# Seven products of halves for eight of the 22 tiles of the up product, and low parts made by an adding DMA

## The chip, the cores and the metric

One core of one Trainium2 chip runs the whole kernel, one layer of a network on 512 positions of 1024 features. The metric is the device time of one execution in microseconds. The kernel before and the changed one are compared by the median of several runs on the same chip. Engines are named as in the profile: PE is TensorE, DVE VectorE, ACT ScalarE, POOL GpSimd, SP SyncE.

## The reference

All is float32. The part that is changed is the first product of the convolutional gated MLP (`h @ w_up`), which is the longest stage of the layer:

```python
x1 = x + rmsnorm_post_mix(W_out(sig(a_ret) * W_ret_o(retention(h)) + sig(a_sgu) * W_sgu_o(sgu(h))))
y  = x1 + rmsnorm_post_ffn(conv_gated_mlp(rmsnorm_pre_ffn(x1)))

def _conv_gated_mlp(h, w_up, conv_w, conv_b, w_down):      # h: 512 x 1024
    hid = h @ w_up                                         # 512 x 5632
    hid = depthwise_conv(hid, conv_w, width=3, pad=1) + conv_b   # along the positions
    a, b = jnp.split(hid, 2, axis=-1)                      # 2 x 2816
    return (jax.nn.gelu(a) * b) @ w_down                   # 2816 x 1024
```

## The kernel before

**Numbers in two parts.** A float32 product is taken in three passes of TensorE: each operand `a` is split into a high part `ah` (a copy in the format that TensorE reads) and a low part `al = a - ah`, and `mm3` adds `ah*bh`, `ah*bl` and `al*bh` in PSUM. The high copy is made by ACT (`copy`), the subtraction by DVE (`split`).

**Weights.** All weights lie in one array `wall` of 146 blocks of 128 x 1024 (512 KB each), in the order of their use. The list `units` says in which form each is needed. `w_get` hands out the next unit and, as it does, prepares units further on (`w_unit`, with `LOOK` as the reach): it loads the block into one of 4 `raw` tiles by a DMA of SP's queue and makes the parts in one of 9 slots of the pool `w4`. A plain block (`w_block`) takes two slots, `wh` and `wl`: an ACT copy 128x1024 and a DVE subtraction 128x1024.

**Products of halves.** For two products of the first half of the kernel (U and the gates), and for the down product, a product of 2 x 2 blocks is taken in seven products of halves instead of eight, with sums and differences of the operands in place of the operands (the algorithm of Strassen in Winograd's form). `w_form` makes the seven forms of weights (B11, B21, T1 to T4, B22, each 128x512 with its two parts): T1 and T3 are sums on DVE, T2 and T4 sums on POOL. `x_forms` makes the forms S1 to S4 of the activations. The class `Pair` takes the seven products, in three parts between which other products can stand, with 84 matmuls 128x256 and three accumulators.

**The up product.** Its 5632 features are 44 blocks of 128, in 22 tiles `i` of two blocks (`e = 2i` of `a`, `2i + 1` of `b`). `f_block` computes one block: 8 slices `k` of the input times 3 passes, 24 matmuls 128x512 into one PSUM bank. `conv` takes the bank with one ACT step (`cv`, the middle tap and the bias) and two DVE steps (the taps of the neighbours), `gated` takes the gelu on ACT and the product `gp` on DVE. After every second tile up to the thirteenth, `down_forms` makes the forms of two `gp` for the down product: eight DVE steps of differences and splits.

**The start of the stage.** The 512 positions are handled as four groups `t` of 128. `norms(t)` computes the rows `x1` and their normalised `xn`; `turn(t)` transposes them (`transpose`, 8 on PE), and writes for each `k` 128 columns of the operand: `h2h` by ACT straight from PSUM, `h2l` by one DVE step from PSUM and `h2h`. The first four blocks are computed in halves of 256 positions (`early(e, 0)` and `early(e, 1)`), the first half before the last two turns are there.

**Order.** The program lists the operations in the order of the text; a scheduler then arranges each engine's queue, so that operations of several stages stand mixed. An engine runs its queue in order and waits for semaphores. The DMA queues are SP's (all weight blocks) and POOL's (`x1` written and read).

The plain split and the whole weight block, as they stand:

```python
    def split(hi, lo, src):
        copy(hi, src)
        nc.vector.tensor_sub(lo, src, as32(hi))
```

Of the kernel before, what the change touches and what calls it, by code (L numbers as in the profile page):

```python
# [12 lines left out]
AF = mybir.ActivationFunctionType  # L13
ALU = mybir.AluOpType

P = 128
# [17 lines left out]
DP = 9  # L34
WHOLE = NF - 2 * DP
EAGER = 7

PRE, FFNG, LNG, LNB = 0, 8, 16, 24
CW, CB = 32, 32 + 3 * 2 * NF
# [4 lines left out]
def tile_block(ctx: ExitStack, tc, xT, x, wall, par, cs, decay, wsp, bsp, gpost, gffn, out):  # L44
# [11 lines left out]
    def blk(dt=F32, n="blk", shape=(P, S)):  # L56
        return sb.tile(list(shape), dt, tag="blk", bufs=NBLK, name=nm(n))

    def tmp(n="tmp", shape=(P, S)):
        return sb.tile(list(shape), F32, tag="tmp", bufs=6, name=nm(n))  # L60
# [16 lines left out]
    def as32(t):  # L77
        return t.bitcast(F32)
# [6 lines left out]

    RES1 = NW - 22 - 44
    RES0 = RES1 - RES_OUT
    units = []
    i = 0
    while i < NW:  # L90
        pair = [(f, i) for f in ("B11", "B21", "T1", "T2", "T3", "T4", "B22")]
        if U0 <= i < GATE0:
            units += pair
            i += 2
        elif GATE0 <= i < GATE1:
            units += pair[:4] + [("blk", i + 2)] + pair[4:] + [("blk", i + 3)]
            i += 4
        elif i == DOWN0:
            for _ in range(2):
                pairs = [[("q", i + j), ("t", i + j)] for j in range(DP)]  # L100
                whole = [[("blk", i + DP)], [("blk", i + DP + 1)]]
                for u in pairs[:4] + whole[:1] + pairs[4:6] + whole[1:] + pairs[6:] if i == DOWN0 else pairs + whole:
                    units += u
                i += DP + WHOLE // 2
        else:
            units.append(("blk", i))
            i += 1
# [8 lines left out]
    def w_block(i):  # L116
        raw = raw_tile() if i else raw0
        resident = RES0 <= i < RES1
        if i > 0:
            nc.sync.dma_start(raw, wall[i])  # L120
        if resident:
            hi, lo = [], []
            for c in range(2):
                h_, l_ = blk(F32R, "wh"), blk(F32R, "wl")
                split(h_, l_, raw[:, c * S : (c + 1) * S])
                hi.append(h_)
                lo.append(l_)
        else:
            at = 48 if i >= DOWN0 else 0
            hi, lo = slot("wh", at), slot("wl", at)  # L130
            if i == 0:
                pieces = [slice(0, P), slice(P, S), slice(S, 2 * S)]
                for f in pieces:
                    if f.start:
                        nc.sync.dma_start(raw[:, f], wall[i, :, f])
                    (nc.vector.tensor_copy if f.start == 0 else copy)(hi[:, f], raw[:, f])
                for f in pieces:
                    nc.vector.tensor_sub(lo[:, f], raw[:, f], as32(hi[:, f]))
            else:
                split(hi, lo, raw)  # L140
        return hi, lo
# [21 lines left out]
    def w_down(form, i):  # L163

        if form == "q":
            raw = w_raw["q"] = raw_tile()
            nc.sync.dma_start(raw, wall[i])
            raw = raw[:, : 3 * 256]
        else:
            b, raw = w_raw["q"], raw_tile()  # L170
            two = "p (n c) -> p n c"
            nc.vector.tensor_tensor(
                out=raw[:, :512].rearrange(two, n=2), in0=b[:, :512].rearrange(two, n=2),
                in1=b[:, None, 768:].to_broadcast([P, 2, 256]), op=ALU.add,
            )
            nc.vector.tensor_add(raw[:, 512:768], raw[:, :256], b[:, 256:512])
            nc.vector.tensor_add(raw[:, 768:], raw[:, 512:768], b[:, 512:768])
        w = 768 if form == "q" else 1024
        hi, lo = slot("dh", 48, w), slot("dl", 48, w)
        split(hi, lo, raw)  # L180
        return hi, lo

    def w_unit(u):
        return w_block(u[1]) if u[0] == "blk" else w_down(*u) if u[0] in "qt" else w_form(*u)

    def w_size(u):
        return 2 if u[0] in ("blk", "q", "t") else 1

    def w_get(look=LOOK):

# [29 lines left out]
    def col(i):  # L220
        return part[:, i : i + 1]
# [55 lines left out]
    T0, T1 = slice(0, 256), slice(256, 512)  # L277
    forms = {n: [] for n in ("S1", "S2", "S3", "S4")}

    def x_forms(k):  # L280

        a, b = xg[k], xg[k + 4]
        s_ = blk(n="xs")
        nc.vector.tensor_sub(s_[:, T0], a[:, T1], b[:, T1])
        nc.vector.tensor_sub(s_[:, T1], s_[:, T0], a[:, T0])
        nc.vector.tensor_sub(a[:, T0], a[:, T0], a[:, T1])
        nc.vector.tensor_add(a[:, T1], b[:, T0], s_[:, T1])
        for names, s_ in (("S1", "S2"), s_), (("S3", "S4"), a):
            h_, l_ = blk(F32R, "sh"), blk(F32R, "sl")
            split(h_, l_, s_)  # L290
            for n, t in zip(names, (T0, T1)):
                forms[n].append((h_[:, t], l_[:, t]))
# [344 lines left out]
    class Pair:  # L637


        def __init__(self, func, alloc):  # L640
            self.func, self.t = func, [alloc(), alloc()]
            self.b = [ps() for _ in range(3)]

        def product(self, b, act, first, w=None):
# [9 lines left out]
                    )  # L654
            return o

        @staticmethod
        def x(first, t):
            return lambda k: (xh[first + k][:, t], xl[first + k][:, t])

        @staticmethod
        def s(n):
            return lambda k: forms[n][k]

        def part1(self):
            c0, c1 = self.t
            o = self.product(0, self.x(0, T0), True)
            copy(c0[:, T0], o)
            o = self.product(1, self.x(4, T0), True)
            v.tensor_add(c0[:, T0], o, c0[:, T0])  # L670
            self.product(2, self.s("S1"), True)
            o = self.product(0, self.s("S2"), False)
            copy(c1[:, T0], o)
            v.tensor_mul(c0[:, T0], c0[:, T0], rbc[:, T0])

        def part2(self):
            c0, c1 = self.t
# [5 lines left out]
        def part3(self):  # L683
            c0, c1 = self.t
            o = self.product(0, self.x(4, T1), False, self.w[0])
            v.tensor_mul(c0[:, T1], o, rbc[:, T1])
            nc.scalar.activation(out=c0, in_=c0, func=self.func)
            o = self.product(2, self.s("S4"), False, self.w[1])
            v.tensor_sub(c1[:, T0], o, c1[:, T0])
            v.tensor_mul(c1, c1, rbc)  # L690
            nc.scalar.activation(out=c1, in_=c1, func=self.func)


    nc.sync.dma_start(wst, wsp)
# [5 lines left out]
    copy(rws, rw)  # L700
    uT, late = [], None
    for j in range(KD // 2):
        p = Pair(AF.Gelu_apprx_tanh, lambda: blk(n="u"))
        p.part1()
        if late:
            late.part3()
        p.part2()
        late = p
        uT += p.t
# [32 lines left out]


    def gated_pair(ah, al, late=None):
        p = Pair(AF.Sigmoid, lambda: tmp("sig"))
        p.part1()
        if late:
            late.part3()
        o = [f_block(ah, al, KD)]
        p.part2()  # L750
        o.append(f_block(ah, al, KD, p.part3))
        return zip(o, p.t)
# [64 lines left out]


    gpm = bcast(gpost, "gpm")
    h2h, h2l = [], []  # L820
    x1 = [[dp_.tile([P, S], F32, tag=f"x1_{t}{n}", name=f"x1_{t}{n}") for n in range(2)] for t in range(NT)]
    for k in range(KD):
        h2h.append(blk(F32R, "h2h"))
        h2l.append(blk(F32R, "h2l"))

    def norms(t, acc):

# [26 lines left out]
    def turn(t, zs):  # L854
        c = slice(t * P, (t + 1) * P)
        for n in range(2):
            p = ps()
            for f in range(4):
                nc.tensor.transpose(p[:, f * P : (f + 1) * P], zs[n][:, f * P : (f + 1) * P], ident)
            for f in range(4):  # L860
                k = 4 * n + f
                pf = p[:, f * P : (f + 1) * P]
                nc.scalar.activation(  # L863
                    out=h2h[k][:, c], in_=pf, func=AF.Copy, scale=col(FFNG + k)
                )
                v.scalar_tensor_tensor(
                    out=h2l[k][:, c], in0=pf, scalar=col(FFNG + k), in1=as32(h2h[k][:, c]),
                    op0=ALU.mult, op1=ALU.subtract,
                )

    EARLY = 4
    early_w, early_o = [], []
# [72 lines left out]
            "S3": (th[:, T0], tl[:, T0]), "S4": (th[:, T1], tl[:, T1]),  # L945
        })

    for i in range(NF):
        cc = []
        for s_ in range(2):  # L950
            e = 2 * i + s_
            o = early_o[e] if e < EARLY else f_block(h2h, h2l, KD)
            cc.append(conv(o, e))
        gated(*cc)
        if i % 2 and i // 2 < EAGER:
            down_forms(i // 2)

# [145 lines left out]
def _inter(a, b):  # L1105
    return np.stack([a, b], 1).reshape(2 * a.shape[0], *a.shape[1:])
# [7 lines left out]
    ], 1)  # L1114


def _gates(a, w):

    return np.concatenate([_two(a), _parts(w, 8, P).reshape(4, 2, P, 1024)], 1).reshape(16, P, 1024)
# [79 lines left out]
```

## Time and profile before

| | |
|---|---|
| Three runs | 842.24, 843.88 and 848.6 us, median 843.88 us |
| Profiled execution | 841.63 us, span 839.8 us, mean granted clock 0.997 |
| TensorE busy | 827.2 us (98%) |
| DVE, ACT, POOL busy | 615.1 us (73%), 401.5 us (48%), 76.0 us (9%) |
| DMA | 93.19 MB, mean 111 GB/s |

The span reaches from the first instruction to the last; 1.8 us of the profiled execution's time lie outside it. A row of a group reads: line, engine, operation, output and inputs by name, shapes, count | busy time, mean ns of one | idle time of the engine before them and what ended it. Lines such as L82 belong to a helper (here `split`). A piece of the chain reads: start, length, engine or queue, what, count. In the timeline a row is the start, the duration, the engine and the instruction.

### The profile page before, as it was taken

What the parts mean: (1) busy time and instruction counts of PE and PEld (TensorE: products, weight loads), DVE (VectorE), ACT (ScalarE), POOL (GpSimd) and SP (SyncE); (2) the same over time, 40 slices, a digit from 0 to 9 for tenths busy, and PEclk for the clock granted to TensorE, in tenths of its full rate; (3) what the DMA queues carried; (4) which work ended last, traced back from release to release, by engine and by line L of the source; (5) the groups of instructions that cost most, each with busy time, mean ns of one, the idle gap of its engine ahead of it and who ended that gap; (6) DMA issues with size and microseconds to landing.
All of it is one profiled execution on the core that took longest, in us unless ns stands there. A gap on an engine that the chain in (4) does not pass through costs nothing.

```text
span 839.8 us, 12386 instructions
## 1 busy us (share of the span) xinstructions
PE 827.2 (98%) x4864; PEld 731.3 (87%) x4864; DVE 615.1 (73%) x996; ACT 401.5 (48%) x649; POOL 76.0 (9%) x87
## 2 busy tenths in 40 slices
PE   8999999999999999999999999999999999999995
PEld 6888888888899999999988898888888888999995
DVE  5689898877897776867665767667777556886956
ACT  5635445545664533444444664444444333643531
POOL 0010000102221111132211200000000000000001
PEclk9999999999999999999999999999999999999998
DMA  7733222213233332323457123323222221242532
GB/s 266 265 114 101 76 76 76 75 51 101 87 100 103 101 101 101 101 78 102 149 163 287 66 85 101 101 100 101 97 85 95 100 76 50 80 135 100 159 132 101
DMA packets 29243, 93.19 MB, mean 111 GB/s; under 512 B 3392, under 2 KB 4032, under 8 KB 29184
## 3 DMA queue, kind: packets, MB, share of 16 engines
q1 hardware_dynamic: 26928, 86.85, 31.1%
q0 software_dynamic: 1392, 4.46, 1.5%
q10 hardware_dynamic: 864, 1.09, 0.4%
q8 instruction: 38, 0.62, 0.3%
q14 instruction: 21, 0.17, 0.1%
HBM read 88.19 MB, written 4.19 MB: 110 GB/s over the span
## 4 chain that ended last, share of the span: by engine, by line
PE 96%; DVE 1%; DMA 1%; issue 1%; ACT 0%; POOL 0%; DVEq 0%; SPq 0%; POOLq 0%; ACTq 0%
PE ps L204 16%; PE ps L203 16%; PE ps L205 16%; PE ps L651 14%; PE ps L977 10%; PE ps L465 5%; PE ps L464 5%; PE ps L466 5%; PE ps L798 2%; PE ps L796 2%; PE ps L797 2%; PE ps L993 2%; PE ps L721 1%; DMA raw<-wall 1%; PE ps L264 1%
## 5 line engine op out<-in xcount | busy, mean ns | idle before, releaser
L82 DVE TENSOR_TENSOR wl<-raw,wh 128x1024 fp32r<-128x1024 f32 (+1 forms) x109 | 128.2, 1184 | 100.0 <-PE ps L204 63.7
L205 PE MATMUL ps<-h2h,wl 128*128 128x512 f32 (+1 forms) x384 | 142.3, 371 | 0.0
L204 PE MATMUL ps<-h2l,wh 128*128 128x512 f32 (+1 forms) x384 | 142.2, 371 | 0.0
L203 PE MATMUL ps<-h2h,wh 128*128 128x512 f32 (+1 forms) x384 | 142.2, 372 | 0.0
L75 ACT ACTIVATE wh<-raw 128x1024 fp32r<-128x1024 f32 (+2 forms) x111 | 109.8, 998 | 37.7 <-DMA raw<-wall 18.1
L75 ACT ACTIVATE wf<-raw 128x512 fp32r<-128x512 f32 x84 | 50.8, 627 | 73.5 <-issue 30.2
L203 PEld LDWEIGHTS ps<-h2h,wh 128*128 128x128 f32 x384 | 72.1, 188 | 12.8 <-ACT h2h L863 0.3
L204 PEld LDWEIGHTS ps<-h2l,wh 128*128 128x128 f32 x384 | 72.2, 188 | 12.6
L205 PEld LDWEIGHTS ps<-h2h,wl 128*128 128x128 f32 x384 | 72.2, 188 | 12.3
L82 DVE TENSOR_TENSOR wf<-raw,wf 128x512 fp32r<-128x512 f32 x84 | 65.8, 799 | 19.9 <-ACT wf L75 19.6
L906 ACT ACTIVATE cv<-ps,part 128x512 f32<-128x512 f32 x44 | 34.4, 781 | 87.9 <-PE ps L205 87.9
L464 PE MATMUL ps<-wh,xh 128*128 128x512 f32 x192 | 75.0, 391 | 0.0
L465 PE MATMUL ps<-wl,xh 128*128 128x512 f32 x192 | 74.9, 390 | 0.0
L466 PE MATMUL ps<-wh,xl 128*128 128x512 f32 x192 | 74.8, 390 | 0.0
L651 PE MATMUL ps<-sh,wf 128*128 128x256 f32 x384 | 72.8, 280 | 0.0
L651 PEld LDWEIGHTS ps<-sh,wf 128*128 128x128 f32 x384 | 60.9, 188 | 0.7 <-ACT u L75 0.2
L977 PE MATMUL ps<-dh,fh 128*128 128x256 f32 x216 | 60.3, 279 | 0.0
L977 PE MATMUL ps<-dl,fh 128*128 128x256 f32 x216 | 60.2, 279 | 0.0
L977 PE MATMUL ps<-dh,fl 128*128 128x256 f32 x216 | 60.2, 279 | 0.0
L651 PE MATMUL ps<-xh,wf 128*128 128x256 f32 x288 | 54.6, 281 | 0.0
L651 PE MATMUL ps<-sl,wf 128*128 128x256 f32 x192 | 53.6, 279 | 0.0
L82 DVE TENSOR_TENSOR dl<-raw,dh 128x768 fp32r<-128x768 f32 (+1 forms) x36 | 39.2, 1091 | 18.7 <-PE ps L204 7.9
(290 smaller groups left out, 1851.7 us busy)
## 6 DMA issues: line engine op xcount, KB each, us to landing
raw<-wall SPq DMA_DIRECT2D x145, 512.0 KB, 3.4
x<-x SPq DMA_DIRECT2D x24, 256.0 KB, 5.8
xT<-xT SPq DMA_DIRECT2D x8, 256.0 KB, 5.5
x<-x POOLq DMA_DIRECT2D x8, 256.0 KB, 2.3
xT<-xT POOLq DMA_DIRECT2D x4, 256.0 KB, 3.8
out<-zg SPq DMA_DIRECT2D x4, 256.0 KB, 2.0
out<-zs ACTq DMA_DIRECT2D x3, 256.0 KB, 2.0
cs<-cs SPq DMA_DIRECT2D x2, 256.0 KB, 4.1
```

Source lines behind the costliest of these rows:

```text
L75: nc.scalar.activation(out=o, in_=i, func=AF.Copy)
L82: nc.vector.tensor_sub(lo, src, as32(hi))
L203: nc.tensor.matmul(o, ah, bh, start=start, stop=False)
L204: nc.tensor.matmul(o, ah, bl, start=False, stop=False)
L205: nc.tensor.matmul(o, al, bh, start=False, stop=stop)
L464: nc.tensor.matmul(acc[t], xh[k][:, c], wh[:, f], start=k == 0, stop=False)
L465: nc.tensor.matmul(acc[t], xh[k][:, c], wl[:, f], start=False, stop=False)
L466: nc.tensor.matmul(acc[t], xl[k][:, c], wh[:, f], start=False, stop=k == KD - 1)
L651: nc.tensor.matmul(o, w_[:, c], a_, start=first and k == n == 0, stop=k == 3 and n == 2, skip_group_check=True,)
L796: nc.tensor.matmul(o, ah, bh, start=k == 0, stop=False)
L906: nc.scalar.activation(out=c, in_=o, func=AF.Identity, scale=col(CW + 3 * m + 1), bias=col(CB + m))
L977: nc.tensor.matmul(o, a_[:, c], w_[:, f], start=j == t == i == 0, stop=j == DP - 1 and i == 2 and n not in (M2, M3, M4), skip_group_check= ...
```

## The change

`COUPLES` are the tiles (3, 4), (5, 6) to (17, 18) of the up product. In each, the first tile is one `Pair` with forms of `h2`, a new plain copy of the operand (eight tiles), and the second two `f_block`s, one after the first part of the pair and one after the second. Weights of the first tile are laid out on the host as the four halves (`_up`). The second tile's blocks are `sum` units: ACT copies the high part, ACT writes minus the block into the low tile, and a DMA on POOL's queue adds the block of `wall` onto it. `turn` writes `h2`, and after an odd `t` splits 256 columns of it. `x_forms` runs for four `k` on `h2`. `down_forms` moves to tiles 3, 7, 11, 15, 18, 19 and 20. The classes' scale becomes optional, since the up product has none.

```diff
+UP0 = DOWN0 - 2 * NF
+COUPLES = [(i, i + 1) for i in range(3, 19, 2)]
...
+        elif i == UP0 + 2 * COUPLES[0][0]:
+            for a, b in COUPLES:
+                pair = [(f, UP0 + 2 * a) for f in FORMS]
+                units += pair[:4] + [("sum", UP0 + 2 * b)] + pair[4:] + [("sum", UP0 + 2 * b + 1)]
+            i = UP0 + 2 * COUPLES[-1][1] + 2
...
+    def w_sum(i):
+
+        raw = raw_tile()
+        nc.sync.dma_start(raw, wall[i])
+        hi, lo = slot("wh"), slot("wl")
+        copy(hi, raw)
+        nc.scalar.activation(out=lo, in_=raw, func=AF.Copy, scale=-1.0)
+        nc.gpsimd.dma_start(lo, wall[i], accum_op=ALU.add)
+        return hi, lo
...
-                pf = p[:, f * P : (f + 1) * P]
                 nc.scalar.activation(
-                    out=h2h[k][:, c], in_=pf, func=AF.Copy, scale=col(FFNG + k)
+                    out=h2[k][:, c], in_=p[:, f * P : (f + 1) * P], func=AF.Copy, scale=col(FFNG + k)
                 )
-                v.scalar_tensor_tensor(
-                    out=h2l[k][:, c], in0=pf, scalar=col(FFNG + k), in1=as32(h2h[k][:, c]),
-                    op0=ALU.mult, op1=ALU.subtract,
-                )
+                if t % 2:
+                    d = slice((t - 1) * P, (t + 1) * P)
+                    split(h2h[k][:, d], h2l[k][:, d], h2[k][:, d])
...
-    for i in range(NF):
-        cc = []
-        for s_ in range(2):
-            e = 2 * i + s_
-            o = early_o[e] if e < EARLY else f_block(h2h, h2l, KD)
-            cc.append(conv(o, e))
-        gated(*cc)
-        if i % 2 and i // 2 < EAGER:
-            down_forms(i // 2)
+    def tile_done(i, o):
+        gated(*(conv(t, 2 * i + s_) for s_, t in enumerate(o)))
+        if i < COUPLES[-1][1]:
+            if i % 4 == 3:
+                down_forms(len(dforms))
+        elif len(dforms) < EAGER:
+            down_forms(len(dforms))
+
+    for k in range(4):
+        x_forms(k, h2[k], h2[k + 4], h2forms)
+    couples = dict(COUPLES)
+    i = 0
+    while i < NF:
+        if i in couples:
+            p = Pair(None, lambda: tmp("c"), (h2h, h2l, h2forms))
+            p.part1()
+            o = [f_block(h2h, h2l, KD)]
+            p.part2()
+            o.append(f_block(h2h, h2l, KD, p.part3))
+            tile_done(i, p.t)
+            tile_done(i + 1, o)
+            i += 2
+        else:
+            o = []
+            for e in (2 * i, 2 * i + 1):
+                o.append(early_o[e] if e < EARLY else f_block(h2h, h2l, KD))
+            tile_done(i, o)
+            i += 1
```

More of the change, by code (lines that the diff above doesn't have):

```diff
@@ L87, in tile_block @@
     RES0 = RES1 - RES_OUT
+    FORMS = ("B11", "B21", "T1", "T2", "T3", "T4", "B22")
     units = []
@@ L90, in tile_block @@
     while i < NW:
-        pair = [(f, i) for f in ("B11", "B21", "T1", "T2", "T3", "T4", "B22")]
+        pair = [(f, i) for f in FORMS]
         if U0 <= i < GATE0:
@@ L181, in w_down @@
         return hi, lo
+    def w_sum(i):
[6 more added lines that the diff above has]
+        return hi, lo
     def w_unit(u):
-        return w_block(u[1]) if u[0] == "blk" else w_down(*u) if u[0] in "qt" else w_form(*u)
+        if u[0] in ("blk", "sum"):
+            return (w_block if u[0] == "blk" else w_sum)(u[1])
+        return (w_down if u[0] in "qt" else w_form)(*u)
     def w_size(u):
-        return 2 if u[0] in ("blk", "q", "t") else 1
+        return 2 if u[0] in ("blk", "sum", "q", "t") else 1
     def w_get(look=LOOK):
@@ L278, in tile_block, with x_forms @@
     forms = {n: [] for n in ("S1", "S2", "S3", "S4")}
-    def x_forms(k):
-        a, b = xg[k], xg[k + 4]
+    def x_forms(k, a=None, b=None, forms=forms):
+        a, b = a or xg[k], b or xg[k + 4]
         s_ = blk(n="xs")
@@ L637, in tile_block, with __init__ @@
     class Pair:
-        def __init__(self, func, alloc):
-            self.func, self.t = func, [alloc(), alloc()]
+        def __init__(self, func, alloc, a=None, scale=None):
+            self.func, self.t, self.scale = func, [alloc(), alloc()], scale
+            self.h, self.l, self.forms = a or (xh, xl, forms)
             self.b = [ps() for _ in range(3)]
@@ L655, in product, with x, s @@
             return o
[L657 to L663, printed above, removed]
+        def x(self, first, t):
+            return lambda k: (self.h[first + k][:, t], self.l[first + k][:, t])
+        def s(self, n):
+            return lambda k: self.forms[n][k]
         def part1(self):
@@ L673, in part1 @@
             copy(c1[:, T0], o)
-            v.tensor_mul(c0[:, T0], c0[:, T0], rbc[:, T0])
+            if self.scale is not None:
+                v.tensor_mul(c0[:, T0], c0[:, T0], self.scale[:, T0])
         def part2(self):
@@ L685, in part3 @@
             o = self.product(0, self.x(4, T1), False, self.w[0])
-            v.tensor_mul(c0[:, T1], o, rbc[:, T1])
-            nc.scalar.activation(out=c0, in_=c0, func=self.func)
+            if self.scale is None:
+                copy(c0[:, T1], o)
+            else:
+                v.tensor_mul(c0[:, T1], o, self.scale[:, T1])
+                nc.scalar.activation(out=c0, in_=c0, func=self.func)
             o = self.product(2, self.s("S4"), False, self.w[1])
             v.tensor_sub(c1[:, T0], o, c1[:, T0])
-            v.tensor_mul(c1, c1, rbc)
-            nc.scalar.activation(out=c1, in_=c1, func=self.func)
+            if self.scale is not None:
+                v.tensor_mul(c1, c1, self.scale)
+                nc.scalar.activation(out=c1, in_=c1, func=self.func)
     nc.sync.dma_start(wst, wsp)
@@ L702, in tile_block @@
     for j in range(KD // 2):
-        p = Pair(AF.Gelu_apprx_tanh, lambda: blk(n="u"))
+        p = Pair(AF.Gelu_apprx_tanh, lambda: blk(n="u"), None, rbc)
         p.part1()
@@ L744, in gated_pair @@
     def gated_pair(ah, al, late=None):
-        p = Pair(AF.Sigmoid, lambda: tmp("sig"))
+        p = Pair(AF.Sigmoid, lambda: tmp("sig"), None, rbc)
         p.part1()
@@ L819, in tile_block @@
     gpm = bcast(gpost, "gpm")
-    h2h, h2l = [], []
+    h2h, h2l, h2 = [], [], []
+    h2forms = {n: [] for n in ("S1", "S2", "S3", "S4")}
     x1 = [[dp_.tile([P, S], F32, tag=f"x1_{t}{n}", name=f"x1_{t}{n}") for n in range(2)] for t in range(NT)]
@@ L824, in tile_block @@
         h2l.append(blk(F32R, "h2l"))
+        h2.append(blk(n="h2"))
     def norms(t, acc):
@@ L946, in down_forms @@
         })
-    for i in range(NF):
-        cc = []
-        for s_ in range(2):
-            e = 2 * i + s_
-            o = early_o[e] if e < EARLY else f_block(h2h, h2l, KD)
-            cc.append(conv(o, e))
-        gated(*cc)
-        if i % 2 and i // 2 < EAGER:
-            down_forms(i // 2)
+    def tile_done(i, o):
[19 more added lines that the diff above has]
+            i += 2
+        else:
+            o = []
[3 more added lines that the diff above has]
+            i += 1
     UNITS = (("q", 0, "A11"), ("q", 2, "A12"), ("q", 1, "S4"), ("t", 0, "S1"), ("t", 2, "S2"), ("t", 1, "S3"), ("t", 3, "A22"))
@@ L1114, in _two, with _up @@
     ], 1)
+def _up(a):
+    for i, _ in COUPLES:
+        b, c = a[2 * i].reshape(P, 2, S), a[2 * i + 1].reshape(P, 2, S)
+        a[2 * i : 2 * i + 2] = np.stack([
+            np.concatenate([b[:, 0], c[:, 0]], -1), np.concatenate([c[:, 1], b[:, 1]], -1),
+        ])
+    return a
 def _gates(a, w):
@@ L1166 @@
         _rows(i["w_out"]),
-        _inter(_parts(up[:, :DFF], NF, P), _parts(up[:, DFF:], NF, P)),
+        _up(_inter(_parts(up[:, :DFF], NF, P), _parts(up[:, DFF:], NF, P))),
         _down(i["w_down"]),
```

## The prediction

> **What bounds the kernel now.** I read the page first, then the table of busy time by stretches of 20 us over the stage that is changed, then the chain of waits for the cadence of TensorE.
>
> ```profile
> span 839.8 us, 12386 instructions
> PE 827.2 (98%) x4864; PEld 731.3 (87%) x4864; DVE 615.1 (73%) x996; ACT 401.5 (48%) x649; POOL 76.0 (9%) x87
> PE 96%; DVE 1%; DMA 1%; issue 1%; ACT 0%; POOL 0%; DVEq 0%; SPq 0%; POOLq 0%; ACTq 0%
> ```
>
> TensorE is busy for 98% of the span and makes 96% of the chain that ends last, so only fewer or narrower matmuls, or new holes in PE, can move the time.
>
> ```profile
> core 0: us, PE busy (x) PEld busy (x) DVE busy (x) ACT busy (x) POOL busy (x), PEclk, DMA share, GB/s
> 370.00:390.00 20.00, 20.00 (x127) 18.07 (x126) 14.46 (x21) 8.56 (x15) 5.11 (x5) 1.00 0.28 97
> 480.00:500.00 20.00, 19.98 (x167) 19.74 (x166) 12.78 (x27) 11.47 (x26) 1.69 (x3) 1.00 0.20 61
> 500.00:520.00 20.00, 20.00 (x97) 16.86 (x96) 17.46 (x27) 12.31 (x17) 0.00 (x0) 1.00 0.38 125
> 600.00:620.00 20.00, 20.00 (x90) 16.57 (x89) 14.92 (x22) 9.47 (x13) 0.00 (x0) 1.00 0.28 88
> 720.00:740.00 20.00, 20.00 (x172) 20.00 (x171) 19.97 (x34) 12.71 (x20) 0.00 (x0) 1.00 0.30 93
> ```
>
> The up product is the middle of this table. PE is full there, at the full clock (1.00), DVE has 5 us spare in 20, ACT 10, POOL does nothing and DMA is at 0.28. So there is room to pay for halves with vector work, except at two places: DVE is at 17.46 of 20 where the up product starts and at 19.97 of 20 where it ends.
>
> **What the change removes from PE.** A couple of tiles was 4 blocks of 24 matmuls 128x512. Tile `a` now has 7 products of 12 matmuls 128x256 (84), tile `b` keeps 48 wide ones. The cadence of both kinds:
>
> ```profile
> 368.89 5.66 PE ps L651 x48
> 389.75 5.66 PE ps L651 x48
> 410.60 5.65 PE ps L651 x48
> 501.68 0.40 PE L203 MATMUL ps<-h2h,wh 128*128 128x512 f32 x1
> 719.47 19.79 PE ps L977 x168
> ```
>
> (The first three and the last are pieces of the chain: start, length, what, count; the fourth is the timeline.) Wide: the 40 blocks of 24 between 501.68 and 719.47, 217.8 us / 960 = 0.2269 us. Narrow: 5.66/48 = 0.1179, and 19.79/168 = 0.1178. A couple before is 96 x 0.2269 = 21.78 us. The gate product already runs 84 narrow and 48 wide in turn, and its period is 389.75 - 368.89 = 20.86 us (20.85 for the next). So a couple saves 0.92 by the period, or 84 x 0.1178 + 48 x 0.2269 = 20.79 and 0.99 by the counts. Eight couples: 7.4 to 7.9, taken 7.5 us. That is 0.9% of the time and a ceiling: nothing else leaves PE's queue.
>
> **What it adds in the steady state.** The nearest rows are those of the gate product and of the up product itself.
>
> ```profile
> L82 DVE TENSOR_TENSOR wl<-raw,wh 128x1024 fp32r<-128x1024 f32 x38 | 46.5, 1224 | 60.6 <-PE ps L204 59.5 <-issue 1.0
> L82 DVE TENSOR_TENSOR wf<-raw,wf 128x512 fp32r<-128x512 f32 x75 | 59.7, 812 | 15.7 <-ACT wf L75 15.4
> L155 DVE TENSOR_TENSOR raw<-raw,raw 128x512 f32<-128x512 f32 x10 | 9.1, 909 | 0.7 <-DMA raw<-wall 0.7
> L913 DVE SCALAR_TENSOR_TENSOR cv<-ps,part,cv 128x511 f32<-128x511 f32 x42 | 31.4, 749 | 1.1
> L922 DVE TENSOR_TENSOR gp<-cv,cv 128x512 f32<-128x512 f32 x21 | 14.5, 692 | 0.8
> L936 DVE TENSOR_TENSOR fs<-fs,gp 128x256 f32<-128x256 f32 x7 | 3.0, 425 | 0.2
> L75 ACT ACTIVATE wh<-raw 128x1024 fp32r<-128x1024 f32 x37 | 38.9, 1051 | 0.0
> L906 ACT ACTIVATE cv<-ps,part 128x512 f32<-128x512 f32 x42 | 32.8, 781 | 85.8 <-PE ps L205 85.8
> L75 ACT ACTIVATE wf<-raw 128x512 fp32r<-128x512 f32 x75 | 45.4, 627 | 68.5 <-issue 30.2 <-PE ps L204 21.1 <-PE ps L651 12.8
> L75 ACT ACTIVATE sig<-ps 128x256 f32<-128x256 f32 x24 | 9.0, 377 | 8.3 <-PE ps L651 8.3
> L156 POOL TENSOR_TENSOR raw<-raw,raw 128x512 f32<-128x512 f32 x10 | 18.3, 1832 | 88.3 <-DVE raw L154 63.1 <-DMA raw<-wall 16.9 <-ACT wf L75 4.4
> L158 POOL TENSOR_TENSOR raw<-raw,raw 128x512 f32<-128x512 f32 x11 | 14.2, 1291 | 49.6 <-DVE wf L82 49.6
> ```
>
> DVE, one couple before: 4 `wl` x 1.224 + 8 convolution steps x 0.75 + 2 `gp` x 0.69 + one set of `down_forms` (up to tile 13; eight steps, 5 x 0.42 and 3 x 0.68, 4.1) = 16.4 of 21.78. After: the four `wl` go; 7 `wf` x 0.812, the sums T1 and T3 (0.9 and, by the width, 0.7), 3 combinations 256 wide x 0.42, the same convolution and `gp`, and `down_forms` in every second couple (2.1) = 18.0 of 20.86, 86%. A couple that has its `down_forms` has 20.1. ACT: 7 x 0.627 + 4 x 1.051 (a high and a negated copy for each adding block; the negated one has no row and is priced as `wh`) + 4 x 0.781 + 2 gelu x 0.63 + 4 copies out of PSUM x 0.377 + 1.1 for half a `down_forms` = 15.6, 75%. POOL: 3.1 us of sums and two DMA issues. All of this is covered by PE as long as each form arrives before its product. Walking one couple in the order in which the program issues, the tightest forms (S2's and S3's) come 1.3 to 3.6 us early: priced at 0, and at about 1 us a couple if DVE loses those margins.
>
> **The adding DMA** is in no row. It reads 512 KB of `wall` onto a tile that holds minus the rounded raw block. The nearest rows:
>
> ```profile
> raw<-wall SPq DMA_DIRECT2D x145, 512.0 KB, 3.4
> x<-x POOLq DMA_DIRECT2D x8, 256.0 KB, 2.3
> xT<-xT POOLq DMA_DIRECT2D x4, 256.0 KB, 3.8
> ```
>
> Below: 3.8, a POOL load of half the size. Above: two of these end to end, 7.6, since an add must also fetch what it adds to. I take 5.5. It stands on POOL's queue behind T2 and T4, up to 3.1 us, and its issue. In the walk, ACT ends the negated copy of the first adding block 17.7 us into a couple and PE needs it at 27.0; for the second 25.8 and 33.9. Less POOL, 6.5 to 8 us are left for the landing: no stall at 5.5, at most 1 us each at 7.6. A DMA also lengthens the queue: 6 transfers a couple where 4 were, 3.1 MB in 20.86 us, 151 GB/s, against the 125 that the table shows in the fullest stretch.
>
> The Trainium skill (DMA: Bandwidth & Descriptors, section on the anatomy of a DMA on the gpsimd path) fits 2.0 us plus bytes over 436 GB/s, 3.2 us for 512 KB, and gives no price for the adding kind. The plain load in the trace takes 3.4; by the page the first adding block, below, would stall 0.7 us, not 3.0.
>
> **Where it starts.** Here nothing is spare. Before, each `h2h` is an ACT step straight from PSUM, and DVE's `h2l` follows it, each time 128 columns. Now ACT writes `h2` and, only after the odd `t`, copies 256 columns, so the second turn puts 16 ACT steps where 8 were, and DVE subtracts 256 wide.
>
> ```profile
> 476.63 0.28 PE L203 MATMUL ps<-h2h,wh 128*128 128x256 f32 x1
> 476.89 0.60 ACT L807 ACTIVATE junk<-ps 128x512 f32<-128x512 f32 x1
> 478.13 0.35 DVE L866 SCALAR_TENSOR_TENSOR h2l<-ps,part,h2h 128x128 fp32r<-128x128 f32 x1 [0.36 <-ACT h2h L863]
> 478.50 0.75 DVE L838 SCALAR_TENSOR_TENSOR z<-ps,qr,gpm 128x512 f32<-128x512 f32 x1
> 477.92 0.55 POOL L815 TENSOR_TENSOR qr<-qs,nhalf 128x1 f32<-128x1 f32 x1 [1.66 <-DVE qs L812]
> 489.64 2.73 ACT L863 ACTIVATE h2h<-ps,part 128x128 fp32r<-128x128 f32 x7 [3.93 <-PE ps L859]
> 490.06 0.74 PE ps L203 x4
> ```
>
> (Timeline rows; the last is a piece of the chain.) Four places, each walked from these rows with the new order of instructions:
>
> 1. The first early block starts at 476.63 and takes a slice of `h2` every 0.36 us (three narrow matmuls), so it wants the last at 479.2. In the new order ACT does the `h2` and `h2h` of the second turn in turn with two `junk` squares (0.6 each) of the next norm between the last ones: the eighth `h2h` ends near 479.9. On DVE the eighth `h2l` now stands behind `qs` and `z`, and `z` waits for POOL's `qr`, 0.55 after the second square: 480.4, then 0.75 and 0.42 give 481.45. Stall 2.2 us (0, if PE's queue gives it other matmuls, to 3.5).
> 2. After the fourth turn (489.17, eight transposes) the first block starts 0.4 after ACT's first `h2h`. Now two `h2` steps of 0.3 come before each copy, 0.33: about 0.95 us for two slices in place of 0.7. Stall 1.1 us (0.6 to 2.5).
> 3. DVE then builds the forms of `h2`: 4 x (4 x 0.42 + 2 x 0.69) = 12.2 us, in the stretch in which it already has 17.46 of 20; `down_forms` for the first pair leaves (-4.1). The walk leaves the second block of tile 2 late by 0.3 and the form T1 of the first couple by 0.6: 0.9 us (0 to 4).
> 4. The first adding block: ACT's negated copy ends at about 518.9, POOL's T4 goes before it, issue at 519.6, landing 525.1 by my 5.5, against a need at 522.1; both move on together with what 1 to 3 lose. Stall 3.0 us (1.3 at 3.8, 5.1 at 7.6).
>
> Sum 7.2 us, 1.9 to 15.1. What is queued behind the wait in 1 is the rest of turn 2 on DVE: two `x1` sums and the `xn` of the next turn, whose transposes PE reaches only 9 us later.
>
> **Where it ends.** In 720:740 DVE is full with the forms of the down product. Three sets of `down_forms` now stand at tiles 18, 19 and 20, where none stood (the last was at tile 13): about 38 us of DVE work in the last 35.4 us of the stage. The walk has the first form that can be late 1.5 to 2.4 us early, before 2.9: priced 0, up to 2.
>
> **Sum.** -7.5 + 7.2 + 0 = -0.3 on the profiled execution's 841.63 us, 841.3. The three runs have 842.24, 843.88 and 848.6; the middle of all four executions is 843.06, so I forecast 842.8 us.
>
> **A rule that speaks against it.** POOL's T2 and T4 come into a stage in which POOL did nothing:
>
> ```profile
> 374.35 2.32 DVE L82 TENSOR_TENSOR wl<-raw,wh 128x1024 fp32r<-128x1024 f32 x1
> 373.92 1.67 POOL L156 TENSOR_TENSOR raw<-raw,raw 128x512 f32<-128x512 f32 x1 [2.18 <-ACT wf L75]
> ```
>
> The subtraction that is 1.224 alone takes 2.32 when it starts within POOL's sum: DVE stood still until POOL's end at 375.59, 1.24 less the overlap of starting. The mean 0.812 of `wf` (against 0.69 alone) has a share of this in it already. If all of T2 and T4 stopped DVE, a couple would be at 18.0 + 3.1 = 21.1 of 20.86. The Trainium skill (SBUF — State Buffer, section "Who interferes with whom") says that a DVE instruction with two SBUF inputs contends with a GpSimd instruction that reads SBUF, and that the loser waits for the whole of it; by that rule the trace agrees.
>
> **Rivals.**
>
> - *The start is hidden.* For it: PE's order can move products, and DVE idles between turns in the rows above (12.78 of 20). Against: the eighth `h2l` is behind `z` by its order, not by a time. The time is 843.06 - 7.5 = 835.6, 0 to 1.4 of stalls either way: 834.5 to 837.
> - *The adding DMA is slow, slower than before.* One mechanism: an add lands in 10 us or more, above the 6.5 to 8 that the order leaves. For it: it fetches twice, has no row, and two are on one POOL queue with T2 and T4 before them, and the subtraction's cover, DVE, is not used. Against: DMA is at a third of its time. It decides from 8 us on; at 10 each of 16 blocks costs 1 to 2 us once the first has landed (16 to 32 in all, 8 to 16 if only the tighter one of a couple shows), so with 4 us of the other stalls 843.06 - 7.5 + 4 + 16 = 856, 848 to 872.
> - *DVE becomes the bound.* At 86%, with 20.1 of 20.86 where `down_forms` falls and POOL's blocking on top: 20.1 + 2 - 20.86 = 1.3 late in four couples, 5 us, and the tail's 2: 842.8 + 7 = 850, 846 to 855. Against: the gate product runs POOL's sums with DVE at 14.46 of 20 and keeps its 20.86.
> - *The halves don't give it.* The seven products of `h2` would have to run slower than the gate's, of the same shape: nothing in the rows says so. The time would be 843.06 + 7.2 = 850.
>
> **How the numbers follow.** Forecast (stalls of 3 to 11 us at the start, nothing after; 838 to 847): 0.47. Start hidden: 0.17, of which 0.07 below 835.4. Slow adding DMA: 0.19. DVE the bound: 0.13, a half of it over 852.3. No gain from halves, or two mishaps together: 0.04. 1% (835.4 and 852.3) is about what a measurement of this kernel tells from no change. Faster by over 1%: 0.07. Slower: 0.19 less 0.01, plus 0.07, plus 0.03 = 0.28. The rest, 0.65, within. The range takes in the hidden start at its lower end and the middle of the slow DMA at the upper, 834.5 to 856.
>
> **What would show it right or wrong.** The chain of waits: pieces of 48 narrow matmuls at a period of 20.8 to 20.9 us over the eight couples (saving right), with no DMA or DVE pieces between. The idle time of PE before the early block near 479, 490 and at the first adding block: 2.2, 1.1 and 3.0 us. The issue rows: a `wl` DMA on POOL of 512 KB, landing in 3.8 to 7.6. DVE at some 17 of 20 in the couples. Wrong: PE waiting in each couple for `wl` (slow DMA), or for `wf` and the ends of convolutions (DVE), or a total below 835 with no wait at 479.

## The result, and the profile after

The changed kernel takes 850.86 us (median of 20 runs, 846.96 to 857.45) against 843.47 us for the kernel before (20 runs): ratio 1.0082, 95% interval 1.0062 to 1.0102. It is slower by 0.8%, where I had forecast 842.8 us, as good as no change: the difference is under 1%, but clear of the noise. On the chip of some later runs it came out at 1.0070 (1.0051 to 1.0088).

The page of after: the span, the busy times, the chain, and the DMA rows.

```profile
span 847.5 us, 13270 instructions
PE 824.3 (97%) x5152; PEld 739.5 (87%) x5152; DVE 636.0 (75%) x1068; ACT 446.2 (53%) x761; POOL 114.0 (13%) x119
PE 80%; DMA 7%; DVE 5%; issue 4%; ACT 2%; POOL 1%; SPq 0%; DVEq 0%; POOLq 0%; ACTq 0%
...
q0 software_dynamic: 3696, 12.85, 7.3%
...
raw<-wall SPq DMA_DIRECT2D x145, 512.0 KB, 4.2
wl<-wall POOLq DMA_DIRECT2D x16, 512.0 KB, 7.7
```

PE is busy for 2.9 us less than before (a matmul at a lower clock counts as busy for longer), and the span is 7.7 us longer. PE's share of the chain fell from 96 to 80%, and DMA has 7% of it. The new row is the last: the 16 adding DMAs land 7.7 us after their issue.

The up product from the first matmul of the first early block to the last of tile 21 took 242.5 us before (476.63 to 719.09) and 249.9 after (476.19 to 726.07): nearly the whole difference lies in this stage. Its waits on PE in after, in order of their total (what waits, for whom: us in all, times, the longest):

```profile
PE ps L225 <- DMA wl<-wall: 6.9, 4, 4.7
PE ps L224 <- DVE h2l L84: 1.1, 1, 1.1
PE ps L673 <- ACT c L77: 0.7, 1, 0.7
PE ps L223 <- ACT h2h L77: 0.6, 1, 0.6
PE ps L225 <- DVE wl L84: 0.5, 1, 0.5
PE ps L673 <- DVE wf L84: 0.4, 1, 0.4
```

Before, this list is empty for the stage. The first adding DMA is the 4.7. The chain shows it (start, length, what), and what comes behind it:

```profile
519.65 0.69 issue
520.34 8.24 DMA wl<-wall
528.62 0.80 PE ps L225
529.42 0.43 PE ps L223
...
533.26 0.43 PE ps L223
533.69 0.39 PE ps L224
534.08 0.23 PE ps L225
```

A wide matmul takes 0.43 us here in place of 0.23, twelve of them with the first, which is longer: about 2.7 us lost. The table by stretches says why (clock granted, DMA share and GB/s at the end of the row):

```profile
core 0: us, PE busy (x) PEld busy (x) DVE busy (x) ACT busy (x) POOL busy (x), PEclk, DMA share, GB/s
515.00:520.00 5.00, 4.62 (x40) 4.42 (x39) 5.00 (x8) 4.03 (x6) 1.36 (x2) 1.00 0.03 6
520.00:525.00 5.00, 3.25 (x25) 2.61 (x23) 3.83 (x7) 3.95 (x6) 1.40 (x3) 1.00 0.87 212
525.00:530.00 5.00, 1.38 (x3) 1.17 (x4) 1.15 (x2) 0.66 (x2) 0.75 (x1) 0.71 1.05 328
530.00:535.00 5.00, 5.00 (x15) 3.91 (x14) 2.48 (x3) 0.60 (x1) 1.82 (x1) 0.61 0.42 87
```

(At 535 to 540 it is 1.00 again.) The wait let the clock of TensorE fall to a half for (0.29 + 0.39) x 5 x 2 = 6.8 us, and PE looks busy while it catches up. And the DMA share shows the transfer's company: next to nothing moves until 520, then two adding DMAs and four plain loads share the engines.

The saving is there as well. Where no wait falls in, the couples of after run at the period that the gate product had:

```profile
631.26 5.65 PE ps L673 x48
652.12 5.66 PE ps L673 x48
```

20.86 us. So the account of the stage is -7.5 for eight couples and +13 to +14 of losses: early blocks 1.7 to 1.9, the last plain `wl` before the couples 0.5, `wf` and the copies `c` out of PSUM 1.1 to 1.4, the first adding DMA 4.7, the half clock 2.7, three later adding DMAs 2.2 to 2.7 (the smaller number by the list of waits, the larger by the distance of matmul starts). Of the 7.4 that the stage is longer, this leaves 1 to 2 us without a name.

### The profile page after: what moved, and what is told of

Its sections match the earlier page's. It is cut to its first block, busy times and chain, and to the rows that moved or that the text cites. A ratio compares the mean times of both kernels' runs of the same rounds, so it can differ in the third digit from the quotient of the medians.

```text
span 847.5 us, 13270 instructions
## 1 busy us (share of the span) xinstructions
PE 824.3 (97%) x5152; PEld 739.5 (87%) x5152; DVE 636.0 (75%) x1068; ACT 446.2 (53%) x761; POOL 114.0 (13%) x119
## 4 chain that ended last, share of the span: by engine, by line
PE 80%; DMA 7%; DVE 5%; issue 4%; ACT 2%; POOL 1%; SPq 0%; DVEq 0%; POOLq 0%; ACTq 0%
PE ps L673 18%; PE ps L225 10%; PE ps L224 10%; PE ps L223 10%; PE ps L1021 8%; PE ps L484 5%; PE ps L485 5%; PE ps L486 5%; DMA raw<-wall 4%; DMA wl<-wall 3%; PE ps L1037 2%; PE ps L821 1%; PE ps L822 1%; PE ps L823 1%; DVE wf L84 1%
## 5 line engine op out<-in xcount | busy, mean ns | idle before, releaser
L84 DVE TENSOR_TENSOR wf<-raw,wf 128x512 fp32r<-128x512 f32 x140 | 109.0, 792 | 33.5 <-ACT wf L77 33.4
L673 PE MATMUL ps<-sh,wf 128*128 128x256 f32 x640 | 121.8, 280 | 1.1 <-ACT c L77 0.7
L84 DVE TENSOR_TENSOR wl<-raw,wh 128x1024 fp32r<-128x1024 f32 (+1 forms) x77 | 86.7, 1136 | 42.0 <-PE ps L673 16.9
L673 PEld LDWEIGHTS ps<-sh,wf 128*128 128x128 f32 x640 | 101.5, 188 | 2.6 <-ACT c L77 1.1
L225 PE MATMUL ps<-h2h,wl 128*128 128x512 f32 (+1 forms) x256 | 94.3, 369 | 7.4 <-DMA wl<-wall 6.9
L224 PE MATMUL ps<-h2l,wh 128*128 128x512 f32 (+1 forms) x256 | 94.0, 368 | 1.1 <-DVE h2l L84 1.1
L223 PE MATMUL ps<-h2h,wh 128*128 128x512 f32 (+1 forms) x256 | 93.7, 368 | 0.6 <-ACT h2h L77 0.6
L673 PE MATMUL ps<-sl,wf 128*128 128x256 f32 x320 | 89.5, 280 | 0.0
L673 PEld LDWEIGHTS ps<-sl,wf 128*128 128x128 f32 x320 | 61.0, 191 | 0.6
L164 POOL TENSOR_TENSOR raw<-raw,raw 128x512 f32<-128x512 f32 x20 | 34.9, 1746 | 165.2 <-DVE raw L162 110.4
```

The lines of the kernel that those rows point to most:

```text
L164: nc.gpsimd.tensor_tensor(out=w_raw["T2"], in0=w_raw["T1"], in1=w_raw["B22"], op=ALU.add)
L223: nc.tensor.matmul(o, ah, bh, start=start, stop=False)
L224: nc.tensor.matmul(o, ah, bl, start=False, stop=False)
L225: nc.tensor.matmul(o, al, bh, start=False, stop=stop)
L673: nc.tensor.matmul(o, w_[:, c], a_, start=first and k == n == 0, stop=k == 3 and n == 2, skip_group_check=True,)
```

## The experiments

All are timed against the kernel before on the same chip. In the first product there can be a stretch at half clock, between 7 and 16 us from the start, that has nothing to do with the change, and it moves the start of the stage between 476 and 482 us. The row for 10 to 20 us of x8 (below; clock granted 0.77) and of the changed kernel (1.00), which have the same text up to there:

```profile
10.00:20.00 10.00, 10.00 (x36) 8.05 (x35) 8.37 (x16) 8.83 (x13) 0.00 (x0) 0.77 0.89 337
```

```profile
10.00:20.00 10.00, 9.45 (x42) 7.51 (x41) 8.44 (x16) 8.21 (x13) 0.00 (x0) 1.00 0.87 313
```

So beside the ratio of the runs I give the length of the up product in the profiled execution, counted as above, which doesn't see it.

| kernel | up product, us | ratio to before (95%) |
|---|---|---|
| before | 242.5 | 1 |
| changed | 249.9 | 1.0082 (1.0062 to 1.0102) |
| x9 changed, again | 248.6 | 1.0070 (1.0051 to 1.0088) |
| x1 plain load for the add | 243.9 | 1.0013 (0.9993 to 1.0034) |
| x2 DVE subtracts everywhere | 240.8 | 0.9980 (0.9954 to 1.0005) |
| x3 DVE subtracts in the first couple | 240.6 | 0.9989 (0.9963 to 1.0016) |
| x4 turn as before | 241.8 | 1.0011 (0.9987 to 1.0035) |
| x5 adds alone, no halves | 242.5 | 0.9985 (0.9967 to 1.0004) |
| x7 seven couples, from tile 5 | 240.1 | 0.9957 (0.9935 to 0.9978) |
| x8 x7 with DVE's subtraction | 238.8 | 0.9952 (0.9929 to 0.9974) |
| x10 x8 with the turn of before | 236.2 | 0.9917 (0.9891 to 0.9943) |
| x11 x10 with eight couples, to tile 20 | 235.2 | 0.9996 (0.9978 to 1.0014) |

My theory was that the add itself is dear and that all that follows (the waits, the half clock) hangs on it; the rivals were DVE, and the place on POOL's queue.

**x1, the add taken out of the DMA** (this kernel leaves out the addition, so its result is another one).

```diff
-        nc.gpsimd.dma_start(lo, wall[i], accum_op=ALU.add)
+        nc.gpsimd.dma_start(lo, wall[i])
```

> The changed kernel with the adding DMA made a plain load of the same 512 KB on the same queue (the low parts then hold the block itself, so the product is another one). Theory A, the add itself is what is dear (each packet of 4 KB takes 0.31 us where a plain one takes 0.20, and landing is 7.7 us): landing falls to 4 to 5 us, the waits of PE for wl fall from 6.9 to under 2 us, and the stretch at half clock behind the first of them goes; 842 to 845 us, ratio 0.998 to 1.002. Rival B, DVE is late and the DMA only the last to come: ratio 1.006 to 1.008. Rival C, the transfer is issued late on POOL's queue: landing falls but half of the wait stays, ratio 1.003 to 1.005.

The page of x1, DMA rows, then its waits and the chain behind the first load:

```profile
q0 software_dynamic: 3696, 12.85, 4.6%
...
wl<-wall POOLq DMA_DIRECT2D x16, 512.0 KB, 4.8
```

```profile
PE ps L225 <- DMA wl<-wall: 2.5, 1, 2.5
```

```profile
526.01 6.11 DMA wl<-wall
532.12 0.04 issue
532.16 0.50 PE ps L225
...
533.59 0.39 PE ps L224
533.99 0.43 PE ps L225
```

The same bytes on the same queue land in 4.8 us where the adding ones take 7.7. The DMA engines' time says it without the queueing (the rest of this queue, in the kernel before, has a share of 1.5%): the 16 adding transfers took (7.3% - 1.5%) x 847.5 = 49.2 us of all 16 engines, 3.07 us each; the plain ones (4.6% - 1.5%) x 847.1 = 26.3, 1.64 each. An add keeps the engines busy 1.9 times as long. Three of the four waits are gone, the first is 2.5 us instead of 4.7, with half the stretch at half clock (it begins at 533.5, 1.4 us after PE has gone on): the stage is 6.0 us shorter than in the changed kernel. Theory A holds for the size of it, though it had the wait under 2 us and the half clock gone. But a plain load also comes late at the first couple, so rival C is right for a part of that one: it is issued late.

**x2, no adding DMA, DVE subtracts everywhere.**

```diff
-            return (w_block if u[0] == "blk" else w_sum)(u[1])
+            return w_block(u[1])
```

> The changed kernel with the eight whole tiles' low parts made by DVE's subtraction again, as everywhere else: the halves alone, without the adding DMA. Theory A: the waits for wl on a DMA and the half clock go (about 10 us of stalls), DVE takes 2 x 1.22 us more in a couple (20.4 of 20.86): 838 to 843 us, ratio 0.994 to 1.000. Rival B, DVE is the bound: couples of 21.5 us and more, PE waits for wf and wl from DVE, 848 to 856 us, ratio 1.005 to 1.015.

Busy time of x2 in three stretches of couples:

```profile
560.00:580.00 20.00, 20.00 (x129) 18.18 (x129) 16.68 (x25) 12.10 (x20) 4.24 (x3) 1.00 0.32 106
600.00:620.00 20.00, 20.00 (x130) 18.20 (x130) 17.70 (x26) 11.76 (x21) 3.82 (x3) 1.00 0.33 106
640.00:660.00 20.00, 20.00 (x127) 18.06 (x126) 18.11 (x27) 11.41 (x20) 4.29 (x3) 1.00 0.38 131
```

PE is full, DVE is at 16.7 to 18.1 of 20 with the two subtractions that the DMA was to take from it. The rival that DVE is the bound falls: the adding DMA relieves an engine that has room, and costs 9.1 us of the stage (249.9 against 240.8). What is left in x2 is the early blocks' 1.6, 0.9 for `wl` and `wf`, and one wait of 2.2 us for a copy `c` out of PSUM. ACT's timeline shows why:

```profile
537.88 0.63 ACT L77 ACTIVATE wf<-raw 128x512 fp32r<-128x512 f32 x1 [2.21 <-POOL raw L164]
538.42 0.36 ACT L77 ACTIVATE c<-ps 128x256 f32<-128x256 f32 x1
```

The copy stands in ACT's queue behind the copy of the form T2, which waits 2.21 us for POOL's sum.

**x3, DVE subtracts in the first couple alone.**

```diff
-            return (w_block if u[0] == "blk" else w_sum)(u[1])
+            return (w_block if u[0] == "blk" or u[1] < UP0 + 2 * COUPLES[1][0] else w_sum)(u[1])
```

> The changed kernel with DVE's subtraction in the first couple alone; the other seven keep the adding DMA. Theory A: the first add's wait (4.7 us) and the half clock after it (2.8 us) go, the later ones (2.7 us) stay: 842 to 845 us, ratio 0.998 to 1.002. Rival B or C: the same wait comes at the next couple's add, with its half clock: 847 to 851 us, ratio 1.004 to 1.009.

240.6 us, 9.2 less than the changed kernel: the wait does not move to the next couple. No wait for an adding DMA reaches the list, and 0.4 us is lost at one of the 14 (616 us, by the starts of the matmuls): the 2.7 us of later adds, which theory A had staying, went too. So what cost most was the first couple's add, and with it the half clock; a wait of 1.6 us for a copy `c` came in its place.

**x4, the turn of before.** `h2h` and `h2l` straight from PSUM for each 128 columns, and `h2` written after them.

```diff
-                    out=h2[k][:, c], in_=p[:, f * P : (f + 1) * P], func=AF.Copy, scale=col(FFNG + k)
-                )
-                if t % 2:
-                    d = slice((t - 1) * P, (t + 1) * P)
-                    split(h2h[k][:, d], h2l[k][:, d], h2[k][:, d])
+                    out=h2h[k][:, c], in_=pf, func=AF.Copy, scale=col(FFNG + k)
+                )
+                v.scalar_tensor_tensor(
+                    out=h2l[k][:, c], in0=pf, scalar=col(FFNG + k), in1=as32(h2h[k][:, c]),
+                    op0=ALU.mult, op1=ALU.subtract,
+                )
+            pn.append(p)
+        for k in range(KD):
+            nc.scalar.activation(
+                out=h2[k][:, c], in_=pn[k // 4][:, (k % 4) * P : (k % 4 + 1) * P], func=AF.Copy, scale=col(FFNG + k)
+            )
```

> The changed kernel with the turn of before: h2h by ACT and h2l by DVE straight from PSUM, 128 columns each, and h2 written after them by 8 more ACT steps a turn. Theory: the two waits of the early blocks (1.2 and 0.7 us) go and nothing else moves, 1 to 2 us less than the changed kernel, ratio 1.005 to 1.007. Rival: the added ACT steps push the forms of h2 and the first add back by 2 us, and the wait is only moved: ratio 1.008 to 1.011.

Its waits in the stage:

```profile
PE ps L673 <- ACT c L77: 2.0, 1, 2.0
PE ps L225 <- DMA wl<-wall: 1.3, 2, 0.9
PE ps L673 <- DVE sl L84: 0.8, 1, 0.8
```

The two waits at the early blocks are gone, as both sides expected, and 2.1 us come back at the first couple (the copy `c` 0.7 to 2.0, the forms' low part `sl` 0.8): the rival's sign. There is also a stretch at half clock behind these two waits, 3.4 us long, which costs about 1.3 us:

```profile
520.00:525.00 5.00, 2.21 (x14) 1.57 (x13) 5.00 (x7) 3.39 (x7) 1.99 (x2) 0.95 0.62 147
525.00:530.00 5.00, 4.07 (x18) 3.55 (x18) 3.83 (x7) 2.73 (x4) 0.87 (x1) 0.71 0.87 234
```

But the wait for the first add fell from 4.7 to under 1, which neither side had. POOL's timelines of the changed kernel and of x4 have its issue:

```profile
520.34 0.93 POOL L198 DMA_DIRECT2D wl<-wall  x1
```

```profile
521.05 0.94 POOL L198 DMA_DIRECT2D wl<-wall  x1
```

Counted from the start of the stage (476.19 and 480.79), the add is issued after 44.2 us in the one and after 40.3 in the other, and PE comes to it at 47.8 and 46.8, in x4 only because it has been held up by the two waits and the half clock just before. With the other turn the scheduler puts the last forms of `h2` on DVE behind the forms of the first couple's weights, so ACT's negated copy and POOL's T4 come earlier. In all the stage is 8.0 us shorter than in the changed kernel, where I had expected 1 to 2: 1.7 from the early blocks, about 3.5 at the first couple (5.0 lost there in place of 8.5, each with its half clock), 0.5 at the last plain `wl` before the couples, and most of the rest at the later adds (one wait of 0.4 in place of three).

**x9, the changed kernel again, and x5, the adds alone in the kernel before.** x5 makes the low parts of the second tiles' 16 blocks with `w_sum` and leaves all else as it was:

```diff
+SUMS = [DOWN0 - 2 * NF + 2 * b + j for b in range(4, 19, 2) for j in range(2)]
...
-            units.append(("blk", i))
+            units.append(("sum" if i in SUMS else "blk", i))
```

> The changed kernel once more, on the chip of the next three. If the 249.9 us that its up product took (from the first matmul of the first early block to the last of tile 21; 242.4 before) is its own, 247 to 252 us come again, with the wait of 4 to 5 us at the first adding DMA and a stretch at half clock behind it; if that one execution was an outlier, 243 to 246 us.

> The kernel before, with the adding DMA for the low parts of the two blocks of tiles 4, 6, 8 to 18, and no halves. Theory (an add of 512 KB lands in 5.5 us alone and in 8 to 10 us beside two or three plain loads; the couples have five or six transfers in a burst, here four in turn with idle DMA): landing 5.5 to 7 us, PE waits for wl under 2 us in all, up product 242.5 to 245 us. Rival (the adding DMA is too slow anywhere): waits of 1 us and more at most of the 16, 250 us and more.

x9 gave 248.6 us, with 4.4 us at the first add and 6.8 us at half clock: the loss there is the kernel's own. The later adds cost it 0.5 us and not 2.2, so that part is not the same in every execution. Of x5 the DMA row:

```profile
wl<-wall POOLq DMA_DIRECT2D x16, 512.0 KB, 7.6
```

Without one product of halves the adds land in 7.6 us (6.5 to 8.1), not in the 5.5 to 7 that I expected; so the landing is the add's own and not the couples' bursts, and that part of my theory falls. Yet PE waits for none of them, the stage takes 242.5 as before: the plain order leaves more time between ACT's copy and the need. A landing of 7.6 is dear only where less than that is left.

**x7 and x8, the first couple two tiles later,** with the adding DMA and with DVE's subtraction.

```diff
-COUPLES = [(i, i + 1) for i in range(3, 19, 2)]
+COUPLES = [(i, i + 1) for i in range(5, 19, 2)]
```

> The changed kernel with seven couples, the first at tiles 5 and 6 instead of 3 and 4 (two more tiles between the turns and the first product of halves). Theory, that the first add and the forms are late since DVE, ACT and POOL still work off the turns and the forms of h2 there: the waits for wf, c and the first wl (1.5 and 4.7 us) and the half clock (2.8) go, the early blocks' 1.9 us and some 2.7 us of later adds stay, the saving is 6.6: up product 239 to 242 us, ratio 0.994 to 0.999. Rival, that the first add is slow for its own traffic (adding and plain loads together in a burst as the pool of slots turns over from whole blocks to halves): the wait of 4 to 5 us and the half clock come two tiles later, 246 to 249 us.

> The same seven couples with DVE's subtraction for every whole block, no adding DMA. Theory: only the early blocks' 1.9 us are left, up product 242.4 - 6.6 + 1.9 = 237.7 us (237 to 239.5), ratio 0.992 to 0.996. Rival, DVE (20.4 of 20.86 by its rows): PE waits for wf or wl of DVE, 241 us and more.

The waits of x7 in the stage:

```profile
PE ps L224 <- DVE h2l L84: 1.1, 1, 1.1
PE ps L223 <- ACT h2h L77: 0.6, 1, 0.6
PE ps L225 <- DMA wl<-wall: 0.5, 1, 0.5
PE ps L225 <- DVE wl L84: 0.5, 1, 0.5
```

The long wait, the half clock and the waits for `wf` and `c` don't come with two tiles in between, so they belong to the work that is left from the start, not to the first change of weight forms. Of the 2.7 us of later adds that I had staying, 0.5 shows. x8 loses only the start's: 238.8, in the expected range. Between the two lies 1.3 us in the stage and nothing that the ratios can tell.

**x10 and x11.** x8 with the turn of x4; and the same with an eighth couple at tiles 19 and 20 (`range(5, 21, 2)`).

> Seven couples from tiles 5 and 6 on, DVE's subtraction everywhere, and the turn of before (h2h and h2l straight from PSUM, h2 written behind them). Theory: with the forms two tiles away, the 1.9 us at the early blocks go and nothing takes their place, as it did where the first couple stood at tiles 3 and 4: up product 238.8 - 1.9 = 236.9 us (236 to 237.5), ratio 0.990 to 0.994. Rival: ACT's 8 more steps a turn and DVE's 8 hold the convolutions of the early blocks or the forms, and PE waits 1 to 3 us for wf or a bank: 238 to 240 us.

> The same with eight couples, tiles 5 and 6 to 19 and 20. Theory of the saving by count (0.93 a couple wherever it stands): up product 236.0 us (235 to 236.8), ratio 0.989 to 0.993. Rival, DVE at the end of the stage, where the forms of the down product fill it already: PE waits for them at the end or behind it and the eighth couple gives nothing or takes 1 to 3 us, ratio 0.992 to 0.998.

x10 has no wait of PE in the whole up product, 236.2 us, and the ratio 0.9917: it is 0.8% faster than the kernel before. The seven couples save 6.3 us, 0.90 each. x11's stage is shorter still (235.2, that is 0.91 for each of eight), but nearly all that the eight save is lost behind it: from the last matmul of tile 21 to the end, the profiled execution takes 127.7 us, before 120.7. Its waits and a stretch at the seam:

```profile
PE ps L1029 <- ACT dh L77: 2.9, 3, 1.6
PE ps L1029 <- DVE dl L84: 0.9, 1, 0.9
```

```profile
720.00:740.00 20.00, 16.22 (x121) 15.37 (x121) 19.93 (x37) 11.92 (x21) 0.00 (x0) 0.91 0.16 53
```

DVE is at 19.93 of 20 and the weights and forms of the down product come late (`dh`, `dl`), with another stretch at a lower clock. So an eighth couple does not pay at the end of the stage, as the rival said, and it costs more there than the rival had (ratio 0.9996, against 0.992 to 0.998). Whether it pays at the front, with the turn of before and DVE's subtraction, no run shows.

## Why the prediction was wrong

- **The saving** was right: 7.5 forecast; 20.86 per couple in the rows of after, and 0.91 x 8 = 7.3 in the up product of x11, where nothing waits.
- **The start, places 1 and 2**: right in kind. The last `h2l` stands behind `qs`, `qr` and `z` (z at 478.90, h2l at 479.56 in the timeline of after) and costs 1.1, not 2.2, as ACT's steps came 0.26 and 0.31 us apart and everything ended 1.5 us earlier. The second is 0.6 against 1.1.
- **Place 3**: 0.9 forecast, 1.6 to 1.9 measured. The waits for `wl` (0.5) and `wf` (0.4) are the forecast 0.9; the 0.7 for `c` came on top. The copy `c` of a product out of PSUM stands in ACT's queue behind copies of weight forms; I had counted it in ACT's sum and not as something that PE waits for.
- **Place 4, the step that failed.** The adding DMA was put at 5.5 us, between 3.8 and 7.6, by reasoning that an add must fetch twice and then choosing the middle. The runs give 7.7 in the median, just above that upper bound, 8.24 for the first and 9.7 at worst; the value taken was 2.2 us short of the median. At 8.24 in place of 5.5 my own sum gives 5.7 for this place; the rows show 4.7, as there were 3.6 us from issue to need and not the 2.5 of the walk. The slow add is one part of that wait, the late issue the other: with a plain load issued as late (x1), 2.5 us of it are left.
- **The half clock** behind that wait was no term at all, and nothing was said for putting it at nothing: 2.7 us, more than the 1.7 by which the wait itself was mis-sized. The Trainium skill (TensorE: Matmul & The Clock Gate, section Part 1) has the gate halve TensorE's clock after an idle window of about 3.4 us. The 4.7 us wait of after is longer than that; the half clock began about 3 us into it and lasted 6.8 us, two such windows. In x1 a wait of 2.5 us, with one of 0.7 just before it, had one such stretch (3.4 us), in x4 waits of 0.8 and 2.0 us close together had one as well, and in x2 a wait of 2.2 us alone had none. So no single wait as long as the page's window was needed here; how short waits add up, no run separates.
- **Steady state**: 0 forecast, 2.2 to 2.7 lost at three later adds (0.5 in x9, the same kernel), for the same reason; "at most 1 us each at 7.6" was near the right price beside the wrong value (two waits were 0.5 or less, one 1.5). The rival with the slow DMA had 10 us and a stall in each couple: neither came.
- **DVE**: 18.0 of 20.86 forecast, that is 17.3 of 20; the stretches at 560, 600 and 640 have 14.5 to 16.9. It was not the bound, and x2 shows that the subtraction that the DMA replaced would have fitted.

With 7.7 at place 4, the steady state taken from the runs, and the half clock added, the sum is -7.5 + 4.2 + 5.2 + 2.5 + 2.7 = +7.1; the stage measured +7.4. That it comes so near is in part luck: places 1 and 2 cost 1.6 less than forecast, place 3 at least 0.7 more, and 1 to 2 us have no name. The chance that I gave to such an outcome was split: I saw a slow add as an all-or-nothing rival, while what came was an add a little slower than its margin.

## What to carry to other kernels

A transfer that has no row in the profile is to be priced at its upper bound where its margin lies between the bounds, for the loss is one-sided. Look for waits of TensorE that are long or close together: here a wait of 4.7 us cost 2.7 more at half clock behind it, and one of 2.2 us that stood alone cost only itself. And before work is moved off an engine, look whether that engine was in the way: DVE had room here in the middle of the stage, and had none at its start and at its end.

## What was not expected of the hardware

- An adding DMA keeps the DMA engines 1.9 times as long as a plain one (3.07 and 1.64 us for 512 KB), and lands 2.9 us later (7.7 and 4.8) on the same queue.
- A wait of PE of 2.5 us with one of 0.7 before it was enough for 3.4 us at half clock in one kernel (x1, eight matmuls of about 0.43 us), and so were waits of 0.8 and 2.0 us in another (x4), while one of 2.2 us alone had no stretch at half clock behind it in a third (x2).
